# Moving the recurrence's root, scans and operand sums in the mixer stages of a hybrid decoder trunk

## The chip, the core and the metric

The kernel runs on one core of one Trainium2 chip. The time is device time in microseconds from start to end of one execution. In the text PE is the matrix engine, ACT the scalar engine, DVE the vector engine, POOL the general engine (GpSimd) and SP the engine that issues most transfers. PSUM is held in banks of 128 x 512 float32.

## The reference

One layer (DEPTH = 1), 1024 tokens, width 1024, all float32: a norm, two token mixers side by side that are merged by gates, an output projection, then a norm and a squared-ReLU MLP, and a last norm. The change touches the mixers:

```python
h = rms_norm(x, norm_mix)
xa, ga, q, f, v, g, m_a, m_b = split(h @ w_in)
# RG-LRU on blocks of 256 channels
xa = causal_conv4(xa, conv_w, conv_b)
r = sigmoid(xa @ w_r + b_r);  i = sigmoid(xa @ w_i + b_i)
log_a = -8 * r * softplus(-lam);  a = exp(log_a)
u = sqrt(max(-expm1(2 * log_a), 0)) * (i * xa)
h_t = a_t * h_(t-1) + u_t                       # scan over time
y_a = h * gelu(ga)
# HGRN2 on 8 heads of 128, in chunks
q = silu(q);  fg = lb + (1 - lb) * sigmoid(f)
k = (1 - lb) * sigmoid(-f)
o = decayed linear attention(q, k, log fg, v)   # state = decay * state + k v
y_b = rms_norm(o, hg_norm) * silu(g)
y = sigmoid(m_a) * y_a + sigmoid(m_b) * y_b     # then y @ w_out, + x, MLP
```

## The kernel before, in words

Every float32 operand of a product is split into a high part (rounded, by ACT, L87) and a low part (the rest, by DVE, L88), and each product is three matmuls: high by high, low by high and high by low (`mm3`, L130 to L134). A weight tile is loaded by SP (`raw`), split into wH and wL and kept in a ring of six. The splitting of weights is traced with a high priority, so the scheduler of the program places it early on ACT and DVE.

**Stages.** The mixers run in eight stages i = (c, p): two halves of the tokens (c, 512 each) and four pairs of heads (p). `stage(i)` is a generator. Its steps are, in order: the values of the pair before (`v_of(i)`, four blocks tt of 24 matmuls into a bank pv, L350), the projection xa (16 matmul groups in 8 steps), the projection q (8 steps), the first two steps of the projection f, then `rg_lru` (r and i, into banks pr and pi, L430 to L439) and the other six steps of f. A step is six matmuls of 512 columns. `hgrn(i)` holds the attention of stage i and calls `go(n)` between its own blocks on PE, which runs n steps of stage i+1. So the attention of one pair lies between the projections of the next. GO = (24, 5, 1, 1, 2) gives the steps: 24 before the score blocks (own block of 32 matmuls, then after two more steps the blocks of levels 2 and 8, 64 matmuls), 5 before the blocks of 32 and 64, one before the transposes pk of the keys, one before the states pkv (L664), two before the outputs po (L684 to L692). After the last stage `last_stage` has the last values, the projections g and mb, and the transposes of the last output.

**Order.** PE's order in this part is that of the trace (pinned). The order on ACT, DVE and POOL is the scheduler's, fixed when the program is built: each engine runs its own queue strictly in that order.

**Banks.** There are four banks "pj" (all projections, r, i and v), two "sc" and two "hg" (level-8 and 32 scores, pk, pkv, po, the transposes poT of the normalized output and xT_x of the rows of x). A bank is reused when the last reader of its earlier contents is done.

**What the change and the prediction touch.**
- `make_combos` (L303): eight pieces, two in each of stages 4 to 7. POOL forms four sums of the operands (high plus low, L309) and their differences (L313 to L316), ACT copies out the high parts (L322), POOL the low parts (L323), SP stores them. All of it is traced behind `rg_lru`.
- `rg_lru` (L417): sigmoids of r and i on ACT (L424 is the helper that records them, in a fixed order), exp and tanh, then on DVE the product, the root on ACT (L448), two scans on DVE (L456), and one store of 512 KB (L459). The tile xc holds the decay a.
- `q_of` (L461): q times its sigmoid on DVE. `f_of` (L472): the sigmoids f and k (L478, L479); k is scaled by 1 - lb on DVE (L481).
- the end of `hgrn` (L684 to L707): ACT squares each 128 columns of po with a sum (L696) and copies po to `on` (L702); POOL takes the power -0.5 of the mean square (L705, hrs), DVE multiplies `on` by it (L706).
- `on_T` (L369): four transposes of `on` for each head into a bank, scaled by ACT into onT (L376) and stored. It stands at the first v block (tt = 0) two stages later.
- `next_rows` and `transposed` (L296, L158): the four row tiles of the second half of x are loaded, normalized, transposed in stages 1 (after xa), 2, 3 and 4 (third v block), and split into hT10 and hT11 (L87, L88).
- the start of the gates (L1029 to L1044): the first two quads of gate weights are loaded and split, with the loads of the sums t1 and n2 behind the first and T3 and T4 behind the second (`load_combo`); then steps 0 and 3 of both (gX and gZ).

Of the kernel before, what the change touches and what calls it, by code (L numbers as in the profile page):

```python
# [18 lines left out]
P = 128  # L19
# [16 lines left out]
GO = (24, 5, 1, 1, 2)  # L36
# [8 lines left out]
def trunk(ctx: ExitStack, tc: tile.TileContext, x, wts, mlp, pv, gains, mask_f, mask_u, out):  # L45
# [257 lines left out]
    def make_combos(i):  # L303
        k, cut = i // 2, slice(256 * (i % 2), 256 * (i % 2) + 256)
        r = tile_x(f"r{i}").rearrange("p (a b) -> p a b", a=4)
        quarters = ((0, 0), (0, 1), (1, 1), (1, 0))
        for j, (c, h) in enumerate(quarters):
            hi, lo = (hT[c][q][h][:, k, cut].bitcast(F32) for q in range(2))
            ins = G.tensor_tensor(out=r[:, j, :], in0=hi, in1=lo, op=ALU.add)  # L309
            if j == 0:  # L310
                tc.keep_in_program_order(ins)
        b11, b21, b22, b12 = (r[:, j, :] for j in range(4))
        G.tensor_tensor(out=b11, in0=b11, in1=b12, op=ALU.subtract)  # L313
        G.tensor_tensor(out=b12, in0=b22, in1=b12, op=ALU.subtract)
        G.tensor_tensor(out=b22, in0=b11, in1=b22, op=ALU.add)
        G.tensor_tensor(out=b21, in0=b22, in1=b21, op=ALU.subtract)  # L316
        for src, o in ((b11, "t1"), (b22, "n2"), (b12, "T3"), (b21, "T4")):
            if o in ("t1", "T3"):
                st = xt_pool.tile([P, 2, 2, 256], F32, tag="xn", name=f"st{o}{i}", bufs=2)
                at = 0  # L320
            h, lo = (st[:, at, q, :].bitcast(F32R) for q in range(2))
            A.copy(h, src)  # L322
            G.tensor_tensor(out=lo, in0=src, in1=h.bitcast(F32), op=ALU.subtract)  # L323
            nc.sync.dma_start(cd[o][:, :, k, cut], st[:, at])
            at = 1

# [90 lines left out]
    def rg_lru(c, p, xc, xh, xl):  # L417
        wh, wl = next_w()
        nm = f"{c}{p}"
        w, ig, e = (mt(t, f"{t}{nm}", (P, 2, T)) for t in ("rw", "ri", "rr"))  # L420
        last = []
# [25 lines left out]
        V.scalar_tensor_tensor(xc, e, 1.0, w, op0=ALU.add, op1=ALU.mult)  # L447
        on_act(w, w, AF.Sqrt)  # L448
        V.tensor_scalar(xc, xc, -1.0, 1.0, op0=ALU.mult, op1=ALU.add)
        V.scalar_tensor_tensor(w, e, 1.0, w, op0=ALU.add, op1=ALU.mult)  # L450
        V.tensor_tensor(out=ig, in0=ig, in1=w, op=ALU.mult)
        hs = mt("h", f"h{nm}", (P, 2, T))
        for s in range(2):
            u = 2 * p + s
            h = hs[:, s if c == 0 else 1 - s, :]
            V.tensor_tensor_scan(h, xc[:, s, :], ig[:, s, :], hcar[:, u : u + 1], op0=ALU.mult, op1=ALU.add)  # L456
            if c + 1 < NC:
                G.tensor_copy(hcar[:, u : u + 1], h[:, T - 1 : T])
        nc.sync.dma_start(hd[p][:, 2 * c : 2 * c + 2, :], hs)  # L459

    def q_of(c, p, pp):  # L461

        q1 = mt("q1", f"q1{c}{p}", (P, 1536)).rearrange("p (a b) -> p a b", b=3)
        sg = mt("tmp", f"sq{c}{p}", (P, 2, T))
        r2 = lambda a: a.rearrange("p (a b) -> p a b", b=2)
        for s in range(2):
            b = slice(256 * s, 256 * s + 256)
            A.activation(sg[:, s, :], pp[s], AF.Sigmoid)
            V.tensor_tensor(out=q1[:, b, 0:2], in0=r2(sg[:, s, :]), in1=r2(pp[s]), op=ALU.mult)
        return q1  # L470

    def f_of(c, p, pp):  # L472
        ff = mt("f", f"f{c}{p}", (P, 2 * T))
        kk = mt("kk", f"kk{c}{p}", (P, 2 * T))
        for s in range(2):
# [5 lines left out]
            V.tensor_scalar(k, k, omlb[:, u : u + 1], None, op0=ALU.mult)  # L481
# [3 lines left out]
    def hgrn(c, p, got, go):  # L485
        q1, f, kk = got["q1"], got["f"], got["kk"]

        nm = f"{c}{p}"
# [88 lines left out]
        go(GO[0] - 8 * (c + p == 0) - (OWN_BEFORE if c > 0 else 0))  # L577
        pt1 = blocks(kk, lambda k: q1[:, 16 * k : 16 * k + 16, :], "1")
        if c > 0:
            go(OWN_BEFORE)  # L580
# [104 lines left out]
        for s, u in both:  # L685
# [16 lines left out]
            A.copy(on[:, 4 * s : 4 * s + 4, :], po[s].rearrange("p (n d) -> p n d", n=4))  # L702
# [3 lines left out]
        mul(on, on, rs.unsqueeze(2).to_broadcast([P, 8, P]))  # L706
        got["on"] = on  # L707

    gots = [{} for _ in range(NC * NPAIR)]
# [14 lines left out]
    def v_of(i):  # L724
        def between(tt):
            if tt == 0 and i > 1:
                on_T(*where(i - 2), gots[i - 2])
            if tt == 2 and "xn" in gots[i - 1]:
                transposed(gots[i - 1]["xn"], hT[1], i - 1, f"x1{i - 1}")

        yield from v_steps(*where(i - 1), gots[i - 1], between)

    def stage(i):
# [13 lines left out]
        if i == 1:  # L747
            transposed(gots[0]["xn"], hT[1], 0, "x10")
# [8 lines left out]
        for _ in range(2 if i != 1 else 7):  # L757
            next(fs)
            yield
# [4 lines left out]
        yield from rg_lru(c, p, *got["xc"])  # L764
        if i < 4:
            got["xn"] = next_rows(i)
        for k in {4: (0, 1), 5: (2, 3), 6: (4, 5), 7: (6, 7)}.get(i, ()):
            make_combos(k)
# [17 lines left out]
    def last_stage():  # L786
        yield from v_of(NC * NPAIR)
        w = [next_w(), next_w()]
        g2 = []
        for c in range(NC):  # L790
# [3 lines left out]
            for s in range(2):  # L794
                o = g[:, s if c == 0 else 1 - s, :]
                A.activation(o, pp[s], AF.Sigmoid)
                V.tensor_tensor(out=o, in0=o, in1=pp[s], op=ALU.mult)
            yield
# [234 lines left out]
    for q in own[:2]:  # L1033
# [6 lines left out]
        for o in ("t1", "n2") if q == own[0] else ("T3", "T4"):  # L1040
            load_combo(o)
    for step in (0, 3):
        for q in own[:2]:
            gate_step(q, step)  # L1044
    gwork[own[0]]["b"]()
# [376 lines left out]
```

## Time and profile before

| | |
|---|---|
| median of 3 runs | 1621.54 us (1621.21 to 1621.56) |
| the profiled execution | 1626.13 us, its span 1624.3 us |
| PE busy | 1547.5 us, 95% of the span |
| DVE, ACT, POOL busy | 1211.0, 816.2, 148.9 us (75%, 50%, 9%) |
| the mixer stages | 0 to about 611 us of the span |
| DMA | 280.07 MB, mean 172 GB/s |

The profile is of one execution; times inside it are from the start of its span. A row of the timeline gives the start, the length, the engine, the line of the kernel, the operation, out <- in with shapes, and in brackets how long the engine had been idle and what ended that. A row of the waits gives the instruction that waited, what it waited for, and then the sum in us, how often, and the longest. L numbers are lines of the kernel before.

### The profile page before, as it was taken

What the parts mean: (1) busy time and instruction counts of PE and PEld (TensorE: products, weight loads), DVE (VectorE), ACT (ScalarE), POOL (GpSimd) and SP (SyncE); (2) the same over time, 40 slices, a digit from 0 to 9 for tenths busy, and PEclk for the clock granted to TensorE, in tenths of its full rate; (3) what the DMA queues carried; (4) which work ended last, traced back from release to release, by engine and by line L of the source; (5) the groups of instructions that cost most, each with busy time, mean ns of one, the idle gap of its engine ahead of it and who ended that gap; (6) DMA issues with size and microseconds to landing.
All of it is one profiled execution on the core that took longest, in us unless ns stands there. A gap on an engine that the chain in (4) does not pass through costs nothing.

```text
span 1624.3 us, 23115 instructions
## 1 busy us (share of the span) xinstructions
PE 1547.5 (95%) x9072; PEld 1290.7 (79%) x9072; DVE 1211.0 (75%) x1730; ACT 816.2 (50%) x1293; POOL 148.9 (9%) x187
## 2 busy tenths in 40 slices
PE   7999998898988998999999997999999999999998
PEld 6887987787877886888888875788888878888886
DVE  5798676595857744877777379878888898788876
ACT  5655755466564523545444266677766632122113
POOL 1012110516052300000000000000000000000000
PEclk9999999999989899999999999999999999999999
DMA  6323222243332336423236782566666575666652
GB/s 237 104 79 118 84 74 104 70 142 103 112 121 79 130 131 246 156 78 130 78 130 240 266 282 79 218 269 239 246 239 256 231 281 200 260 257 251 260 214 104
DMA packets 71053, 280.07 MB, mean 172 GB/s; under 512 B 7584, under 2 KB 15904, under 8 KB 58016
## 3 DMA queue, kind: packets, MB, share of 16 engines
q1 hardware_dynamic: 67920, 267.58, 44.1%
q10 hardware_dynamic: 3024, 11.01, 1.8%
q8 instruction: 71, 1.16, 0.3%
q14 instruction: 38, 0.31, 0.1%
HBM read 193.63 MB, written 84.93 MB: 171 GB/s over the span
## 4 chain that ended last, share of the span: by engine, by line
PE 76%; DVE 9%; ACT 5%; POOL 4%; issue 3%; DMA 2%; ACTq 0%; POOLq 0%; DVEq 0%; SPq 0%
PE dX L132 4%; PE dX L133 3%; PE dX L134 3%; PE uX L132 3%; PE uX L134 3%; PE uX L133 3%; PE gX L134 3%; PE gX L132 3%; PE gX L133 3%; PE dY L133 2%; PE dY L132 2%; PE dY L134 2%; PE pj_q L132 2%; PE uY L133 2%; PE uY L132 2%
## 5 line engine op out<-in xcount | busy, mean ns | idle before, releaser
L88 DVE TENSOR_TENSOR wL<-raw,wH 128x1024 fp32r<-128x1024 f32 x100 | 123.9, 1239 | 115.4 <-ACT wH L87 113.8
L87 ACT CAST wH<-raw 128x1024 fp32r<-128x1024 f32 x100 | 105.1, 1051 | 89.6 <-PE po L133 37.1
L1331 DVE TENSOR_TENSOR acc<-acc,dX 128x512 f32<-128x512 f32 x128 | 85.0, 683 | 29.5 <-PE dX L134 28.6
L87 ACT CAST wA<-q 128x512 fp32r<-128x512 f32 x46 | 28.5, 621 | 133.7 <-PE dX L134 101.0
L1331 DVE TENSOR_TENSOR acc<-acc,dY 128x512 f32<-128x512 f32 x64 | 43.4, 685 | 15.6 <-PE dY L134 14.5
L134 PE MATMUL po<-wH,y 128*128 128x512 f32 x128 | 50.5, 395 | 0.0
L133 PE MATMUL po<-wL,y 128*128 128x512 f32 x128 | 50.2, 393 | 0.0
L132 PE MATMUL po<-wH,y 128*128 128x512 f32 x128 | 50.1, 392 | 0.0
L1191 ACT ACTIVATE b<-b 128x512 f32<-128x512 f32 x48 | 30.2, 630 | 37.1 <-DVE b L1190 37.1
L155 POOL TENSOR_TENSOR rstd_h<-rstd_h,mhalf 128x1 f32<-128x1 f32 x8 | 5.5, 686 | 396.8 <-DVE rstd_h L154 396.8
L602 POOL TENSOR_SCALAR scT<-dd 32x256 f32<-32x256 f32 x32 | 22.3, 697 | 206.9 <-DVE dd L518 205.4
L88 DVE TENSOR_TENSOR wA<-q,wA 128x512 fp32r<-128x512 f32 x46 | 31.5, 686 | 12.7 <-ACT wA L87 12.5
L402 DVE SCALAR_TENSOR_TENSOR xc<-xp,pvt,xc 128x512 f32<-128x512 f32 x48 | 36.1, 753 | 0.0
L879 DVE TENSOR_TENSOR s<-q,q 128x512 f32<-128x512 f32 x46 | 31.5, 687 | 1.2 <-DMA q<-mlp_in 0.7
L884 DVE TENSOR_TENSOR s<-q 128x512 f32<-128x512 f32 x46 | 31.6, 687 | 0.4
L1192 ACT ACTIVATE b<-b 128x512 f32<-128x512 f32 x48 | 30.0, 630 | 1.1
L132 PE MATMUL pr<-xcH,wH 128*128 128x512 f32 x32 | 14.7, 460 | 16.6 <-ACT rw L424 16.6
L134 PEld LDWEIGHTS po<-wH,y 128*128 128x128 f32 x128 | 24.3, 190 | 5.0
L133 PEld LDWEIGHTS po<-wL,y 128*128 128x128 f32 x128 | 24.2, 189 | 5.1
L132 PEld LDWEIGHTS po<-wH,y 128*128 128x128 f32 x128 | 24.3, 190 | 4.9
L132 PE MATMUL pv<-wH,hT10H 128*128 128x256 f32 x64 | 19.6, 306 | 8.1 <-ACT kk L479 8.1
L134 PE MATMUL uX<-h2B11H,wA 128*128 128x512 f32 x64 | 25.1, 392 | 0.5 <-DVE wA L88 0.5
(2529 smaller groups left out, 5449.1 us busy)
## 6 DMA issues: line engine op xcount, KB each, us to landing
raw<-wts_in SPq DMA_DIRECT2D x96, 512.0 KB, 3.4
q<-mlp_in SPq DMA_DIRECT2D x92, 512.0 KB, 3.5
y<-yd SPq DMA_DIRECT2D x7, 1024.0 KB, 8.3
x<-x_in SPq DMA_DIRECT2D x8, 512.0 KB, 6.0
hd<-h SPq DMA_DIRECT2D x8, 512.0 KB, 2.8
od<-onT ACTq DMA_DIRECT2D x8, 512.0 KB, 2.6
cdT<-stT SPq DMA_DIRECT2D x16, 256.0 KB, 2.7
o<-od SPq DMA_DIRECT2D x4, 1024.0 KB, 6.3
```

Of the source, the lines that this page charges most:

```text
L87: keep(A.copy(h, src))
L88: keep(V.tensor_tensor(out=lo, in0=src, in1=h.bitcast(F32), op=ALU.subtract))
L132: pin(PE.matmul(o, ah, bh, start=first, stop=False, **how))
L133: pin(PE.matmul(o, ah, bl, start=False, stop=False, **how))
L134: pin(PE.matmul(o, al, bh, start=False, stop=last, **how))
L402: V.scalar_tensor_tensor(xc[:, s, :], xp[:, j : j + T], pvt[:, PV_CW + 8 * j + u : PV_CW + 8 * j + u + 1], xc[:, s, :], op0=ALU.mult, op1= ...
L602: G.tensor_scalar(scT[32 * b : 32 * b + 32, :, 32 * b : 32 * b + 32], dd[32 * b : 32 * b + 32, :, :], 1.0, 0.0, op0=ALU.mult, op1=ALU.add,)
L879: V.tensor_tensor(out=sa[:, 0, :], in0=a21, in1=a22, op=ALU.add)
L884: V.tensor_tensor(out=sb[:, 0, :], in0=a21, in1=a11, op=ALU.add)
L1191: A.activation(b[:, at, :], b[:, at, :], AF.Relu, scale=-1.0 if at == 2 else 1.0)
L1192: A.activation(b[:, at, :], b[:, at, :], AF.Square)
L1331: V.tensor_tensor(out=dst, in0=dst, in1=banks[bk, pr], op=op)
```

## The change

- `rg_lru` writes the decay into a tile of its own (a) and leaves the root, the product with it, the scans (now in place) and the stores (two of 256 KB) to a function `tail`. It is called in the next stage: behind the first v block, or in stage 1 behind xa.
- `make_combos` becomes a generator of two parts, sums and copies; the parts are called after xa and after `rg_lru` in stages 4 to 7, and in the last stage.
- GO starts with 26 in place of 24, and in every stage but the first the own block is alone, two steps ahead of the other two.
- f runs four steps ahead of `rg_lru` in place of two.
- q is scaled by 1 - lb, in the instruction that multiplies it by its sigmoid; the scaling of k is gone.
- ACT writes `on` from po, scaled by the power, in eight instructions (Identity, 128 columns each); the copy of po and DVE's product are gone.
- `on_T` stands at the second v block (tt = 1); the row tiles 1, 2 and 3 are transposed in stage 2 (third v block) and stage 3 (first and third).
- The sums t1, n2, T3 and T4 are loaded behind both first quads, and the first gate steps are pinned.

```diff
@@ -33,7 +33,7 @@
 OUT_TILES = 8
 QUADS = 16
 LEVELS = (2, 8)
-GO = (24, 5, 1, 1, 2)
+GO = (26, 5, 1, 1, 2)
 OWN_BEFORE = 2
 
 
@@ -314,15 +314,26 @@
         G.tensor_tensor(out=b12, in0=b22, in1=b12, op=ALU.subtract)
         G.tensor_tensor(out=b22, in0=b11, in1=b22, op=ALU.add)
         G.tensor_tensor(out=b21, in0=b22, in1=b21, op=ALU.subtract)
+        yield
         for src, o in ((b11, "t1"), (b22, "n2"), (b12, "T3"), (b21, "T4")):
             if o in ("t1", "T3"):
                 st = xt_pool.tile([P, 2, 2, 256], F32, tag="xn", name=f"st{o}{i}", bufs=2)
                 at = 0
             h, lo = (st[:, at, q, :].bitcast(F32R) for q in range(2))
-            A.copy(h, src)
+            ins = A.copy(h, src)
+            if o == "t1":
+                tc.keep_in_program_order(ins)
             G.tensor_tensor(out=lo, in0=src, in1=h.bitcast(F32), op=ALU.subtract)
             nc.sync.dma_start(cd[o][:, :, k, cut], st[:, at])
             at = 1
+        yield
+
+    pieces = [make_combos(i) for i in range(8)]
+    piece_parts = [pieces[n // 2] for n in range(16)]
+
+    def combos_on(n):
+        for _ in range(n):
+            next(piece_parts.pop(0))
 
     def project_steps(c, name):
 
@@ -414,10 +425,11 @@
         split(xc, xh, xl)
         return xc, xh, xl
 
-    def rg_lru(c, p, xc, xh, xl):
+    def rg_lru(c, p, got, xc, xh, xl):
         wh, wl = next_w()
         nm = f"{c}{p}"
         w, ig, e = (mt(t, f"{t}{nm}", (P, 2, T)) for t in ("rw", "ri", "rr"))
+        a = mt("h", f"a{nm}", (P, 2, T))
         last = []
 
         def on_act(*a, **k):
@@ -444,19 +456,21 @@
             on_act(w[:, s, :], w[:, s, :], AF.Tanh, scale=sp4[:, u : u + 1])
         V.tensor_tensor(out=ig, in0=ig, in1=xc, op=ALU.mult)
         V.tensor_scalar(w, w, 0.0, None, op0=ALU.max)
-        V.scalar_tensor_tensor(xc, e, 1.0, w, op0=ALU.add, op1=ALU.mult)
-        on_act(w, w, AF.Sqrt)
-        V.tensor_scalar(xc, xc, -1.0, 1.0, op0=ALU.mult, op1=ALU.add)
-        V.scalar_tensor_tensor(w, e, 1.0, w, op0=ALU.add, op1=ALU.mult)
-        V.tensor_tensor(out=ig, in0=ig, in1=w, op=ALU.mult)
-        hs = mt("h", f"h{nm}", (P, 2, T))
-        for s in range(2):
-            u = 2 * p + s
-            h = hs[:, s if c == 0 else 1 - s, :]
-            V.tensor_tensor_scan(h, xc[:, s, :], ig[:, s, :], hcar[:, u : u + 1], op0=ALU.mult, op1=ALU.add)
-            if c + 1 < NC:
-                G.tensor_copy(hcar[:, u : u + 1], h[:, T - 1 : T])
-        nc.sync.dma_start(hd[p][:, 2 * c : 2 * c + 2, :], hs)
+        V.scalar_tensor_tensor(a, e, 1.0, w, op0=ALU.add, op1=ALU.mult)
+        V.tensor_scalar(a, a, -1.0, 1.0, op0=ALU.mult, op1=ALU.add)
+
+        def tail():
+            A.activation(w, w, AF.Sqrt)
+            V.scalar_tensor_tensor(w, e, 1.0, w, op0=ALU.add, op1=ALU.mult)
+            V.tensor_tensor(out=ig, in0=ig, in1=w, op=ALU.mult)
+            for s, u in us:
+                h = ig[:, s, :]
+                V.tensor_tensor_scan(h, a[:, s, :], h, hcar[:, u : u + 1], op0=ALU.mult, op1=ALU.add)
+                if c + 1 < NC:
+                    G.tensor_copy(hcar[:, u : u + 1], h[:, T - 1 : T])
+                nc.sync.dma_start(hd[p][:, (s, 3 - s)[c], :], h)
+
+        got["tail"] = tail
 
     def q_of(c, p, pp):
 
@@ -466,7 +480,10 @@
         for s in range(2):
             b = slice(256 * s, 256 * s + 256)
             A.activation(sg[:, s, :], pp[s], AF.Sigmoid)
-            V.tensor_tensor(out=q1[:, b, 0:2], in0=r2(sg[:, s, :]), in1=r2(pp[s]), op=ALU.mult)
+            u = 2 * p + s
+            V.scalar_tensor_tensor(
+                q1[:, b, 0:2], r2(sg[:, s, :]), omlb[:, u : u + 1], r2(pp[s]), op0=ALU.mult, op1=ALU.mult
+            )
         return q1
 
     def f_of(c, p, pp):
@@ -478,14 +495,13 @@
             A.activation(f, pp[s], AF.Sigmoid)
             A.activation(k, pp[s], AF.Sigmoid, scale=-1.0)
             V.tensor_scalar(f, f, omlb[:, u : u + 1], lb[:, u : u + 1], op0=ALU.mult, op1=ALU.add)
-            V.tensor_scalar(k, k, omlb[:, u : u + 1], None, op0=ALU.mult)
         V.tensor_scalar(ff, ff, F_MIN, 1.0, op0=ALU.max, op1=ALU.min)
         return ff, kk
 
     def hgrn(c, p, got, go):
         q1, f, kk = got["q1"], got["f"], got["kk"]
 
-        nm = f"{c}{p}"
+        nm, first = f"{c}{p}", c + p == 0
         mul = lambda o, a, b: V.tensor_tensor(out=o, in0=a, in1=b, op=ALU.mult)
         dd = mt("dd", f"dd{nm}", (P, 8, 32))
 
@@ -574,9 +590,9 @@
         t4 = nxt.rearrange("p (a b) -> p a b", b=4)
         q4 = qb.rearrange("p a (b c) -> p a b c", c=c1)
         level_q(q4, t4, g1, c1)
-        go(GO[0] - 8 * (c + p == 0) - (OWN_BEFORE if c > 0 else 0))
+        go(GO[0] - (10 if first else OWN_BEFORE))
         pt1 = blocks(kk, lambda k: q1[:, 16 * k : 16 * k + 16, :], "1")
-        if c > 0:
+        if not first:
             go(OWN_BEFORE)
         pt2 = blocks(kb, lambda k: qa[:, k * g0 // 32 : (k + 1) * g0 // 32, 1:7, :], str(c0))
         pt8 = blocks(kc, lambda k: q4[:, k * g1 // 32 : (k + 1) * g1 // 32, 1:7, :], str(c1), "hg")
@@ -699,13 +715,16 @@
                     AF.Square,
                     accum_out=ssq[:, 4 * s + n : 4 * s + n + 1],
                 )
-            A.copy(on[:, 4 * s : 4 * s + 4, :], po[s].rearrange("p (n d) -> p n d", n=4))
         V.tensor_scalar(ssq, ssq, 1.0 / P, EPS, op0=ALU.mult, op1=ALU.add)
         rs = mt("hrs", f"hrs{nm}", (P, 8), bufs=2)
         G.tensor_tensor(out=rs, in0=ssq, in1=mhalf, op=ALU.pow)
-        mul(on, on, rs.unsqueeze(2).to_broadcast([P, 8, P]))
+        for s, _ in both:
+            for n in range(4):
+                j = 4 * s + n
+                A.activation(on[:, j, :], po[s][:, n * P : (n + 1) * P], AF.Identity, scale=rs[:, j : j + 1])
         got["on"] = on
 
+    xn1 = {}
     gots = [{} for _ in range(NC * NPAIR)]
     where = lambda i: divmod(i, NPAIR)
 
@@ -723,10 +742,12 @@
 
     def v_of(i):
         def between(tt):
-            if tt == 0 and i > 1:
+            if tt == 0:
+                gots[i - 1]["tail"]()
+            if tt == 1:
                 on_T(*where(i - 2), gots[i - 2])
-            if tt == 2 and "xn" in gots[i - 1]:
-                transposed(gots[i - 1]["xn"], hT[1], i - 1, f"x1{i - 1}")
+            for n in {(2, 2): (1,), (3, 0): (2,), (3, 2): (3,)}.get((i, tt), ()):
+                transposed(xn1[n], hT[1], n, f"x1{n}")
 
         yield from v_steps(*where(i - 1), gots[i - 1], between)
 
@@ -745,7 +766,10 @@
             pinned[0] = True
         yield
         if i == 1:
-            transposed(gots[0]["xn"], hT[1], 0, "x10")
+            gots[0]["tail"]()
+            transposed(xn1[0], hT[1], 0, "x10")
+        if i > 4:
+            combos_on(2)
 
         def convolve():
             got["xc"] = conv(c, p, xc, xps)
@@ -754,18 +778,18 @@
         got["q1"] = q_of(c, p, pq)
         yield
         fs = hooked(project_steps(c, f"f{c}{p}"), {6: convolve} if i == 1 else {})
-        for _ in range(2 if i != 1 else 7):
+        for _ in range(4 if i != 1 else 7):
             next(fs)
             yield
         if i == 1:
             pf = yield from fs
             got["f"], got["kk"] = f_of(c, p, pf)
             yield
-        yield from rg_lru(c, p, *got["xc"])
-        if i < 4:
-            got["xn"] = next_rows(i)
-        for k in {4: (0, 1), 5: (2, 3), 6: (4, 5), 7: (6, 7)}.get(i, ()):
-            make_combos(k)
+        yield from rg_lru(c, p, got, *got["xc"])
+        for n in ((0,), (1,), (2, 3))[i] if i < 3 else ():
+            xn1[n] = next_rows(n)
+        if i > 3:
+            combos_on(1 if i == 4 else 2)
         if i != 1:
             pf = yield from fs
             got["f"], got["kk"] = f_of(c, p, pf)
@@ -785,6 +809,7 @@
 
     def last_stage():
         yield from v_of(NC * NPAIR)
+        combos_on(2)
         w = [next_w(), next_w()]
         g2 = []
         for c in range(NC):
@@ -795,6 +820,8 @@
                 o = g[:, s if c == 0 else 1 - s, :]
                 A.activation(o, pp[s], AF.Sigmoid)
                 V.tensor_tensor(out=o, in0=o, in1=pp[s], op=ALU.mult)
+            if c == 0:
+                combos_on(1)
             yield
         w = [next_w(), next_w()]
         for c in range(NC):
@@ -1037,11 +1064,13 @@
         if q == own[0]:
             gwork[q]["sums"]()
         gwork[q]["d"]()
-        for o in ("t1", "n2") if q == own[0] else ("T3", "T4"):
-            load_combo(o)
+    for o in ("t1", "n2", "T3", "T4"):
+        load_combo(o)
+    pinned[0] = True
     for step in (0, 3):
         for q in own[:2]:
             gate_step(q, step)
+    pinned[0] = False
     gwork[own[0]]["b"]()
     live["g2"] = gp_tile("b", "g2_0")
     nc.sync.dma_start(live["g2"], g2d)
```

## The prediction

> **What bounds the kernel now.** I read the busy shares first, then the waits of PE, then the granted clock around the longest waits, then the engine each wait names.
>
> ```profile
> PE 1547.5 (95%) x9072; PEld 1290.7 (79%) x9072; DVE 1211.0 (75%) x1730; ACT 816.2 (50%) x1293; POOL 148.9 (9%) x187
> ```
> ```profile
> PE pr L132 <- ACT rw L424: 16.6, 4, 4.2
> ...
> PE pv L132 <- ACT kk L479: 8.1, 4, 2.8
> PE pj_xa L133 <- DVE hT10L L88: 7.0, 1, 7.0
> ...
> PE pj_q L132 <- issue: 4.4, 2, 3.8
> ...
> PE gZ L132 <- ACT onT L376: 2.2, 1, 2.2
> ```
>
> PE is the bound: 95% busy, so a change pays only by what it takes out of PE's idle time or puts in. The waits (total us, times, longest) that lie in the mixers are 16.6 + 8.1 + 7.0 + 3.8 = 35.5 us. Each also costs something after it ends:
>
> ```profile
> 149.00:155.00 6.00, 6.00 (x16) 4.72 (x17) 4.69 (x11) 0.94 (x2) 0.00 (x0) 0.56 0.03 13
> 269.30:274.00 4.70, 4.70 (x12) 3.68 (x13) 2.36 (x10) 0.00 (x0) 0.00 (x0) 0.52 0.00 0
> 314.00:318.50 4.50, 4.50 (x13) 3.56 (x14) 0.00 (x0) 1.68 (x3) 4.42 (x8) 0.62 0.57 200
> 336.20:340.30 4.10, 4.08 (x34) 4.08 (x35) 4.07 (x6) 2.64 (x6) 0.00 (x0) 1.00 0.45 181
> ...
> 455.60:461.50 5.90, 5.90 (x14) 4.64 (x15) 0.00 (x0) 1.68 (x3) 5.74 (x9) 0.50 0.50 178
> 477.90:482.00 4.10, 4.10 (x22) 4.10 (x23) 4.10 (x5) 2.59 (x6) 0.00 (x0) 0.58 0.43 174
> ...
> 549.50:553.60 4.10, 4.10 (x22) 4.10 (x23) 4.10 (x7) 2.61 (x6) 0.00 (x0) 0.59 0.23 90
> ```
>
> These are the stretches behind the gaps (window and its length, busy times of PE, its weight load, DVE, ACT, POOL; the column ahead of the last two is the granted clock). Behind the 3.8 us issue gap PE loses 6.00 × 0.44 = 2.6 us, behind the 7.0 us gap 4.70 × 0.48 = 2.3. Behind a pr gap it loses 5.90 × 0.50 = 2.95 (455.60), behind the first of them 4.50 × 0.38 = 1.7 (314.00). Of the four pv gaps one cost no clock (336.20), two cost 4.10 × 0.42 = 1.7 each, and the one left is taken like them.
>
> Why the four pr gaps: ACT runs its queue in order. One of them, as PE has it and then as ACT and POOL have it:
>
> ```profile
> 455.59 0.79 PE L132 MATMUL pr<-xcH,wH 128*128 128x512 f32 x1 [4.13 <-ACT rw L424]
> ```
> ```profile
> 447.40 0.28 ACT L696 ACTIVATE on<-po 128x128 f32<-128x128 f32 x1
> ...
> 448.32 0.22 ACT L696 ACTIVATION_READ_ACCUMULATOR on<-po 128x1 f32 x1
> 448.57 0.59 ACT L702 COPY on<-po 128x512 f32<-128x512 f32 x1
> 452.95 0.40 ACT L322 CAST stt<-r 128x256 fp32r<-128x256 f32 x1 [3.79 <-POOL r L313]
> ...
> 454.86 0.68 ACT L424 ACTIVATE rw<-pr,pvt 128x512 f32<-128x512 f32 x1
> ```
> ```profile
> 448.89 1.65 POOL L705 TENSOR_TENSOR hrs<-hssq,mhalf 128x8 f32<-128x8 f32 x1 [9.15 <-DVE hssq L703]
> ```
>
> The copies of the operand sums (L322) wait for POOL, and the sigmoid that frees the pr bank (L424) stands behind them until 454.86. The pv gaps have the root ahead of what frees the f bank:
>
> ```profile
> 545.18 1.28 ACT L424 ACT_TABLE_LOAD   x1
> 546.48 1.06 ACT L424 ACTIVATE rw<-rw 128x1024 f32<-128x1024 f32 x1
> 547.55 1.28 ACT L479 ACT_TABLE_LOAD   x1
> 548.85 0.60 ACT L479 ACTIVATE kk<-pj_f 128x512 f32<-128x512 f32 x1
> ```
>
> **What goes.** The sums' copies are traced behind the sigmoids, so the pr waits go: 16.6 us, and the clock after them, 1.7 for the first and 2.95 taken for the other three, 10.5: 27.1 us. The root follows the next chain: 8.1, and three times 1.7: 13.2. The transposes of row tile 3 go one stage earlier, so the 7.0 us wait at stage 4's xa goes with its 2.3: 9.3. The 3.8 us "issue" wait names no releaser and comes after a long run of score blocks; that run is now cut by two steps, and I take it as gone, with its 2.6: 6.4 (none to all; the trace cannot say more). Together **56.0 us**.
>
> **What comes.** (a) Normalization moves from two ACT copies and a DVE product to eight ACT scalings that read PSUM and wait for POOL's power. Let E be when the second po bank is done, 447.35 above (447.40 is the first square on it). The squares end 1.2 later, the power at 450.54, 3.2 after E. ACT then has, ahead of the pr sigmoid, eight scalings of 128x128. No row has that form: a quarter of the 512-wide copy is 0.15, a square and its READ add up to 0.50 (0.28 + 0.22), and four such pairs, overlapped, took 447.40 to 448.54, 0.28 each. I take 0.2 to 0.28, nearest to the pairs: 1.6 to 2.25 us. With the sigmoid's 0.68 the bank is free at E + 5.5 to 6.1. PE wanted it at 451.46 (455.59 less 4.13), E + 4.1. So six stages (2 to 7) stall 1.5 to 2.1 us with the 0.05 from sigmoid to PE; 1.9 taken. The clock loss of 1.7 behind such a gap is taken half the time, 0.85 each. 6 × (1.9 + 0.85) = 16.5 us (6 × 1.5 = 9 to 6 × 3.9 = 23.4).
>
> By the Trainium skill, TensorE: Matmul & The Clock Gate, Part 1, the clock falls only after an idle window of some 3.4 us. By that, (a) would be 5.1 us less and the time about 1601; the row at 477.90 disagrees, 0.58 behind a gap that was at most 2.8, and decides; this gets no chance of its own.
>
> (b) Scores now come two steps of 1.4 us later (GO 26 for 24), so pk follows the end of q's projection, and the copies kT stand behind q's sigmoids.
>
> ```profile
> 507.59 0.58 ACT L634 COPY scT<-sc 64x512 f32<-64x512 f32 x1 [0.33 <-PE sc L628]
> 509.51 0.48 ACT L659 COPY kT<-pk 128x384 f32<-128x384 f32 x1 [1.34 <-PE pk L654]
> ...
> 513.85 1.05 ACT L87 CAST wH<-raw 128x1024 fp32r<-128x1024 f32 x1
> ```
> ```profile
> L664 PE MATMUL pkv<-v,kT x12: 270/275/356, 511.0 to 512.3; 128*128 128x128 f32 x12
> ```
>
> After the scT copy (508.1) ACT now has a table load 1.28, a sigmoid (0.60 long as at 548.85, 0.5 to the next start), a wH cast 0.95, a sigmoid 0.5, then kT 0.48: 511.8, where PE wanted pkv at 511.0. That is 0.8 in hgrn 1 to 3; in 4 to 6 ACT also waits in that stretch for a POOL sum, 1.45; 0.5 in hgrn 7: 2.4 + 4.4 + 0.5 = 7.3 us (0 to 12, with the clock). By the Trainium skill, ScalarE: Activation LUTs, What ACT_TABLE_LOAD costs, a switch is 2.66 us with its drain; by that, (b) would be 7 × 1.38 = 9.7 more and the time about 1615. The rows 545.18 to 546.48 show 1.30 to the next operation and decide; this too gets no chance of its own.
>
> (c) Row tile 2 is now transposed in stage 3 between the first and second v blocks, into both hg banks; poT follows one v block later and needs such a bank. It is free when DVE has written the low parts, which stand in DVE's order behind the whole f chain and now also behind the second half of the recurrence.
>
> ```profile
> 254.92 2.46 DVE L456 TENSOR_TENSOR_SCAN h<-xc,hcar,ri 128x512 f32<-128x512 f32 x2
> 257.29 0.53 DVE L480 TENSOR_SCALAR f<-f,par 128x512 f32<-128x512 f32 x1
> ...
> 263.44 1.23 DVE L88 TENSOR_TENSOR wL<-raw,wH 128x1024 fp32r<-128x1024 f32 x1
> ...
> 268.46 0.70 DVE L88 TENSOR_TENSOR hT10L<-xT_x,hT10H 128x512 fp32r<-128x512 f32 x1
> ...
> 269.39 0.70 DVE L88 TENSOR_TENSOR hT11L<-xT_x,hT11H 128x512 fp32r<-128x512 f32 x1
> ```
> ```profile
> 258.08 1.03 PE L162 MATMUL xT_x<-ident,xn 128*128 128x128 f32 x8
> ```
>
> In before the low parts of tile 3, in the same place a stage later, ended 12.0 us after their transpose (258.08 to 270.1) and 12.8 after the last f operation (257.29). Now two wL (2.5) leave that stretch, and a product, another and the two scans (1.2 + 1.2 + 2.46) enter it: 15.2. The step of PE's time is this:
>
> ```profile
> 608.06 0.39 PE L132 MATMUL mb<-hT11H,wH 128*128 128x512 f32 x1
> 608.29 0.39 PE L133 MATMUL mb<-hT11L,wH 128*128 128x512 f32 x1
> ```
>
> 0.23 a matmul. After E come the second bank's po matmuls and one f step (1.8 to r), 24 matmuls of r and i (5.5), four f steps of six (5.5), two v blocks of 24 half-width matmuls (2.8 each), a transpose (0.9, half of it beside them) and the stall of (a): PE wants poT at about E + 20.5. ACT ends r and i's last sigmoid near E + 9.5, then a table load 1.28, four sweeps of 0.63, a load 1.28, f, k, f with a wH: f at E + 17, so DVE is done at E + 32.5. **12 us** and 2.5 of clock: 14.5 (0, if DVE gets there early, to 16).
>
> (d) The gates. In before t1 and n2 (4 MB) came in while the last projections ran; now all 8 MB of sums follow, on SP's queue, the second quad's load, which waits for a tile that DVE frees.
>
> ```profile
> DMA  0000000899999992000027699999999991019500
> GB/s 0 0 0 0 0 0 10 207 378 408 439 413 418 418 416 96 28 5 0 0 111 290 252 315 423 403 429 424 418 434 418 424 429 71 10 43 373 229 0 0
> ```
> ```profile
> 614.04 0.50 PE L132 MATMUL gZ<-hT01H,wA1234H 128*128 128x512 f32 x1 [2.22 <-ACT onT L376]
> ```
> ```profile
> 615.68 0.69 DVE L88 TENSOR_TENSOR wA<-q,wA 128x512 fp32r<-128x512 f32 x1 [2.83 <-ACT wA L87]
> ```
>
> (40 slices of 580 to 645.) The first step is pinned on wA, ready at 616.4, where before gZ could start at 614.0: 2.4 later. 8.5 MB from 616.4 at about 0.42 MB/us is done by 637 to 639; four pinned steps of 2.7 us hold PE until 627, and the other steps want each operand at about the time it lands. I take +2 us (−1.5 to 6).
>
> **At nothing:** the scaled q (0.05 longer) for the k product gone (2 × 0.48) and the normalizing product gone: about 2 us a stage off DVE, which is 75% busy and off PE's path but in (c); the scan in place and two stores of 256 KB for one of 512, and three row loads of 512 KB a stage earlier on SP, in stretches like 455 to 482 above where DMA is at 0.50 or under; the power's place on POOL, 9% busy. Were DVE's cover gone it would cost those 2 us a stage back. f's two further steps before r stand against two fewer after it, no sum.
>
> Sum of what comes: 16.5 + 7.3 + 14.5 + 2 = **40.3**. Net −15.7 on the profiled execution, 1626.1 to 1610.4. That execution lies 4.6 above the median of the runs, 1621.5, so **1606 us**, −1.0%.
>
> **Rivals.**
> - *The scalings hold the pr banks as long as the sums did* (slower). ACT is in order; if each scaling costs 0.4 to 0.45 rather than 0.2 to 0.28 (the pair of a square and its READ adds up to 0.50), or a wH cast of 1.05 falls between them, the sigmoid ends at E + 7.5 or later. The stall is then 3.6 and the clock loss 2.95 in six stages: 39.3 for 16.5, +22.8: 1629. It decides against the change from 15.7 / 6 = 2.6 us a stage, clock included, over what (a) has. For it: the clock rows; against: 0.28 for such a pair, start to start.
> - *The gates wait for DMA.* If the sums come one after another behind the quad, T3 and T4 would be 5 us late each, with a clock loss: +10, 1616. For it: 0.42 MB/us is the top of the GB/s row. Against: the pinned steps give 10.8 us of cover.
> - *(c) is cheap.* If the f chain runs early, since two wL and 1 us of k products are gone, the wait falls under 2 us: 1593. Against: the 7.0 row is the same wait with less ahead of it.
> - *The gaps stay.* The change does not do what it says if the "issue" wait remains (6.4), (b) drops the clock each time (5) and the pv banks still come late (5): +16, 1622, no change.
>
> **How the numbers follow.** Chances: forecast 0.48 (its own range 1598 to 1613), scalings slow 0.19, gates 0.12, (c) cheap 0.11, gaps stay 0.10. To leave no more than 2 in 10 out, the range goes from 1593 to 1627. A measurement of this kernel can tell about 0.2%, 3.2 us, from no change: faster takes the forecast, the gates, cheap (c), 0.71; same most of the last, 0.08; slower the scalings and the rest, 0.21.
>
> **What would show it.** PE's waits should have no pr wait on L322's place of over 3 us, no pv wait on kk, none at pj_xa; instead pr waits of 1.6 to 2.2 six times, pkv on kT 0.5 to 1.5 seven times, one poT wait of about 12 on hT10L or hT11L, and the gates' first wait near 4.5. It is wrong if the pr waits reach 3.6, if poT does not wait, or if gY or gX wait for transfers.

## The result and the profile after

The changed kernel takes 1645.57 us (median of 4 runs, 1641.66 to 1647.95) against 1621.55 for the kernel before beside it: a ratio of 1.0146 (95% interval 1.0126 to 1.0166), 24 us slower. 1606 was forecast. The profiled execution took 1646.05 us, its span is 1644.3. PE is busy 1549.7 us of it (1547.5 before), so 18 of the 20 us by which the span grew are idle time of PE; the mean granted clock is 0.979 in both profiles.

PE's waits in the changed kernel (what waited, for what: us in total, times, longest):

```profile
PE poT L386 <- DVE hT10L L88: 12.4, 1, 12.4
PE pr L132 <- ACT rw L436: 11.3, 6, 1.9
...
PE sc L644 <- ACT qf L612: 7.5, 3, 2.7
...
PE sc L633 <- DVE qb L505: 5.1, 3, 3.9
...
PE gX L132 <- ACT wA L87: 3.8, 1, 3.8
PE pj_xa L134 <- DVE wL L88: 3.5, 2, 1.8
PE xT_x L162 <- ACT onT L387: 3.4, 1, 3.4
PE pk L670 <- DVE dd L534: 2.6, 1, 2.6
PE pk L670 <- DVE kk L505: 2.3, 2, 1.9
...
PE pkv L680 <- ACT kT L675: 1.9, 3, 0.7
PE g L134 <- DVE wL L88: 1.8, 1, 1.8
```

What the change was to remove is gone: no pr wait of 4 us, no pv wait on kk, none of xa on hT10L, and the issue wait is at most 1.0. What was forecast to come is there as well: pr six times 1.9, poT 12.4, the gates 3.8. But four kinds of waits stand here that the forecast did not have: the scores of 32 and 64 (sc) on qb and qf, the keys' transposes on kk, the next projection on wL, together 7.5 + 5.1 + 2.3 + 3.5 + 1.8 = 20.2 us, and xT_x on onT, 3.4. The one wait of the keys' transposes on dd also grew, from 1.0 to 2.6. Windows behind three of the waits (the granted clock is ahead of the last two columns):

```profile
183.60:188.00 4.40, 4.40 (x12) 3.49 (x13) 0.00 (x0) 1.20 (x2) 0.00 (x0) 0.61 0.04 14
...
212.70:219.00 6.30, 6.30 (x34) 6.30 (x35) 1.46 (x8) 1.37 (x2) 0.00 (x0) 0.59 0.31 125
400.40:404.00 3.60, 3.60 (x16) 2.98 (x17) 0.00 (x0) 1.98 (x3) 0.00 (x0) 1.00 0.04 14
449.00:457.00 8.00, 6.00 (x29) 4.93 (x30) 7.23 (x12) 7.43 (x12) 4.36 (x6) 0.57 0.32 100
```

Behind one pr wait of 1.9 us the clock was low (183.60, 4.40 × 0.39 = 1.7 us lost), behind another it was not (400.40); of the six it was low behind three. The poT wait cost 6.30 × 0.41 = 2.6 behind it; the last window, with a sc wait of 2.4 us in it, has a clock of 0.57.

The new waits begin in DVE. This is its timeline in stage 5, then POOL's and ACT's (start, length):

```profile
439.90 3.28 DVE L413 SCALAR_TENSOR_TENSOR xc<-xp,pvt,xc 128x512 f32<-128x512 f32 x3
...
445.67 2.09 DVE L505 TENSOR_TENSOR qb<-qb,seg 128x256 f32<-128x256 f32 x2
447.68 1.21 DVE L505 TENSOR_TENSOR kk<-kc,seg 128x512 f32<-128x512 f32 x1
448.82 1.20 DVE L505 TENSOR_TENSOR qf<-qb,seg 128x512 f32<-128x512 f32 x1
```
```profile
444.89 1.46 POOL L309 TENSOR_TENSOR r<-hT10H,hT10L 128x256 f32<-128x256 f32 x1
...
448.42 1.05 POOL L315 TENSOR_TENSOR r<-r 128x256 f32<-128x256 f32 x1
```
```profile
449.51 0.40 ACT L323 CAST stt<-r 128x256 fp32r<-128x256 f32 x1 [11.54 <-POOL r L315]
...
450.34 0.61 ACT L612 COPY qf<-qb 128x512 f32<-128x512 f32 x1
```

The sums on POOL now run beside the score chain on DVE, and both are slow. The same two instructions of the score chain and the conv, in stages 4 to 7 (count: shortest/median/longest in ns, first and last start), before and after:

```profile
L489 DVE TENSOR_TENSOR qf<-qb,seg x4: 675/683/690, 359.6 to 573.6; 128x512 f32<-128x512 f32 x4
...
L402 DVE SCALAR_TENSOR_TENSOR xc<-xp,pvt,xc x18: 727/742/884, 356.6 to 509.3; 128x512 f32<-128x512 f32 x18
...
L315 POOL TENSOR_TENSOR r<-r x7: 723/734/738, 320.9 to 534.2; 128x256 f32<-128x256 f32 x7
```
```profile
L505 DVE TENSOR_TENSOR qf<-qb,seg x4: 678/1204/1215, 375.8 to 597.1; 128x512 f32<-128x512 f32 x4
...
L413 DVE SCALAR_TENSOR_TENSOR xc<-xp,pvt,xc x18: 743/1079/1229, 365.9 to 521.9; 128x512 f32<-128x512 f32 x18
...
L315 POOL TENSOR_TENSOR r<-r x8: 730/1052/1610, 330.0 to 588.8; 128x256 f32<-128x256 f32 x8
```

683 ns became 1204, 742 became 1079, POOL's 734 became 1052. All of DVE is busy 1218.3 us, against 1211.0 before, although the change takes 24 instructions off it. In before most of the sums ran right behind the outputs po, in a stretch where DVE had next to nothing to do (0.93 us busy of 4.2 in the pr gap at 451).

### The profile page after: what moved, and what is told of

It is laid out like the page before. It is cut to its first block, busy times and chain, and to the rows that moved or that the text cites. A ratio compares the mean times of both kernels' runs of the same rounds, so it can differ in the third digit from the quotient of the medians.

```text
span 1644.3 us, 23134 instructions
## 1 busy us (share of the span) xinstructions
PE 1549.7 (94%) x9072; PEld 1287.7 (78%) x9072; DVE 1218.3 (74%) x1706; ACT 819.9 (50%) x1341; POOL 190.6 (12%) x187
## 4 chain that ended last, share of the span: by engine, by line
PE 70%; DVE 13%; ACT 6%; POOL 5%; issue 4%; DMA 2%; ACTq 0%; DVEq 0%; POOLq 0%; SPq 0%
PE dX L132 3%; PE dX L133 3%; PE dX L134 3%; PE uX L132 3%; PE uX L134 3%; PE uX L133 3%; PE gX L133 3%; PE gX L132 3%; PE gX L134 3%; PE dY L134 2%; PE dY L133 2%; PE dY L132 2%; PE uY L134 2%; PE uY L132 2%; PE uY L133 2%
## 5 line engine op out<-in xcount | busy, mean ns | idle before, releaser
L1360 DVE TENSOR_TENSOR acc<-acc,dY 128x512 f32<-128x512 f32 x64 | 43.3, 685 | 15.6 <-PE dY L134 14.5
L326 POOL TENSOR_TENSOR stt<-r,stt 128x256 fp32r<-128x256 f32 x16 | 35.3, 2211 | 90.6 <-ACT stt L323 90.6
L712 ACT ACTIVATE on<-po 128x128 f32<-128x128 f32 x64 | 16.8, 276 | 48.4 <-PE po L708 48.4
L413 DVE SCALAR_TENSOR_TENSOR xc<-xp,pvt,xc 128x512 f32<-128x512 f32 x48 | 40.4, 862 | 0.0
L323 ACT CAST stt<-r 128x256 fp32r<-128x256 f32 x16 | 6.4, 403 | 47.6 <-POOL r L315 47.5
L134 PEld LDWEIGHTS po<-wH,y 128*128 128x128 f32 x128 | 24.0, 188 | 4.9
```

The source lines that it names most:

```text
L134: pin(PE.matmul(o, al, bh, start=False, stop=last, **how))
L413: V.scalar_tensor_tensor(xc[:, s, :], xp[:, j : j + T], pvt[:, PV_CW + 8 * j + u : PV_CW + 8 * j + u + 1], xc[:, s, :], op0=ALU.mult, op1= ...
L1360: V.tensor_tensor(out=dst, in0=dst, in1=banks[bk, pr], op=op)
```

## The experiments

Theory: the sums beside the score chain are the main loss, and the poT wait the second. Rivals: the recurrence's tail lengthens the chain; the order on ACT (a sum's copy that waits for POOL ahead of qf); the two steps of GO. Times are medians; since the runs of before beside the experiments differ (medians 1622.6 to 1624.7), ratios to those beside each are given, and a difference of 0.0100 is 16.2 us.

### The transposes put back in order

```diff
-            if tt == 1:
+            if tt == 0 and i > 1:
                 on_T(*where(i - 2), gots[i - 2])
-            for n in {(2, 2): (1,), (3, 0): (2,), (3, 2): (3,)}.get((i, tt), ()):
+            for n in {(2, 2): (1,), (3, 2): (2,)}.get((i, tt), ()):
...
+        if i == 3:
+            transposed(xn1[3], hT[1], 3, "x13")   # behind xa
```

> The changed kernel with the transposes put back in order: poT at the first v block again, row tile 2 at the third v block of stage 3, row tile 3 behind the xa of stage 3. Theory (the hg banks wait for DVE's low parts): the 12.4 us poT wait and its 13.65 us at half clock (6.8 lost) go, and the 3.4 us wait of xT_x on onT in stage 2 with 1.7 of clock: 1646 falls to about 1622. Rival (the low parts are late wherever they stand): the wait moves to the score block that takes the next hg bank, and only 5 to 10 us are won, 1636 to 1641.

1627.06 us, ratio 1.0013 (1.0002 to 1.0024): 21.6 us less than the changed kernel, of the 24 expected. Its waits have no poT on hT10L; part came back in the scores, whose waits on qb and qf add up to 15.6 us for 12.8:

```profile
PE sc L633 <- DVE qb L505: 9.1, 3, 4.0
...
PE poT L386 <- ACT on L724: 2.7, 2, 1.4
...
PE xT_x L162 <- ACT onT L387: 0.5, 1, 0.5
```

So the order of the transposes is worth about 21 us, and the low parts need not be late wherever they stand. (The 6.8 us of clock in the expectation counts all 13.65 us of low clock, in most of which PE was idle; what PE lost behind the wait is the 2.6 worked out above.)

### POOL's sums left out

The four sums, the four differences and the four low parts of each piece are left out; a DMA fills the tile that the copies read, and both halves stored are the high part.

```diff
-            ins = G.tensor_tensor(out=r[:, j, :], in0=hi, in1=lo, op=ALU.add)
+            nc.sync.dma_start(r[:, j, :], hi)
...
-        G.tensor_tensor(out=b11, in0=b11, in1=b12, op=ALU.subtract)   # and three more
...
-            G.tensor_tensor(out=lo, in0=src, in1=h.bitcast(F32), op=ALU.subtract)
```

> The changed kernel without POOL's work for the operand sums: the tile that the copies read is filled by DMA with one high part, the low parts are not made, and both stored halves are the high part (that part of the computation is left out). Theory (in stages 4 to 7 the sums now run beside the score chain, and POOL and DVE slow each other): DVE's 128x512 products, 1.2 us in that stretch, fall to 0.7, the waits sc on qb 5.1 and qf 7.5, pk on kk 2.3, pj_xa and g on wL 5.3 go with some 10 us of clock: about 1616 to 1620. Rival (the recurrence's tail in the score chain is what makes it late): the waits on qb and wL stay, at most 8 us are won, 1638.

1618.30 us, ratio 0.9963 (0.9950 to 0.9976): 29.7 us less. DVE's instructions stand in the same order as in the changed kernel, and last as they did before:

```profile
L499 DVE TENSOR_TENSOR qf<-qb,seg x4: 684/687/690, 372.2 to 565.7; 128x512 f32<-128x512 f32 x4
...
L407 DVE SCALAR_TENSOR_TENSOR xc<-xp,pvt,xc x18: 729/741/749, 365.8 to 502.8; 128x512 f32<-128x512 f32 x18
```

All waits of sc, wL and kk are gone from the list but 0.3 us on qf; poT 12.4 and pr 11.3 stand as in the changed kernel. DVE's 1706 instructions are busy 1185.6 us in all, where the changed kernel's 1706 are busy 1218.3: POOL's part lengthened them by 33 us. The tail, the two steps and the new place of the own block are all in this kernel, so without POOL's part they do not make the scores late, alone or together.

### Each POOL operation a copy of one operand

Same places, same order on every engine, but each sum, difference and low part is a copy, so that part of the computation is left out.

```diff
-            ins = G.tensor_tensor(out=r[:, j, :], in0=hi, in1=lo, op=ALU.add)
+            ins = G.tensor_copy(r[:, j, :], hi)
```

> The changed kernel with each of POOL's sums, differences and low parts made a copy of one operand, in the same places and order (that part of the computation is left out). If any POOL work beside DVE slows DVE as the sums do: the conv instructions stay near 1.05 us and the products qf near 1.08, 1638 to 1646. If it is POOL's reading of two operands, or its length, that does it (theory): conv falls towards 0.76, qf towards 0.7, the sc and wL waits shrink by half or more, 1620 to 1632.

1620.04 us, ratio 0.9973 (0.9961 to 0.9984): 28 less, nearly as if POOL did nothing.

```profile
L505 DVE TENSOR_TENSOR qf<-qb,seg x4: 686/878/879, 373.6 to 570.7; 128x512 f32<-128x512 f32 x4
...
L413 DVE SCALAR_TENSOR_TENSOR xc<-xp,pvt,xc x18: 727/812/927, 366.1 to 504.3; 128x512 f32<-128x512 f32 x18
...
L309 POOL COPY r<-hT01H x7: 394/397/591, 369.6 to 560.4; 128x256 f32<-128x256 f32 x7
```

A copy is 0.40 us long when undisturbed, the sum 0.73. DVE's products are still 0.2 us longer than 0.68, but no score waits more than 0.3 us for them. So POOL work beside DVE is not harmful as such. Whether what harms is that the sums are longer, or that they read two operands, this run does not tell.

### The order on ACT alone

Each copy of a sum is placed on ACT behind the exp and tanh sweeps of the last recurrence traced, so none of that recurrence's stage stands ahead of the copy of qf.

```diff
             ins = A.copy(h, src)
-            if o == "t1":
-                tc.keep_in_program_order(ins)
+            if rg_done:
+                how = mybir.DependencyInfo(mybir.DependencyClass.NoSync, mybir.DependencyReason.DATA)
+                tc.add_manual_dep(ins.ins, rg_done[-1].ins.name, how, reason="rg_done")
...
+        rg_done.append(last[-1])   # rg_lru, behind the sweeps
```

> The changed kernel with the sums where they are on POOL, but their copies held on ACT behind the recurrence's sweeps of their own stage, so that none stands ahead of the copy of qf. If the order on ACT is the loss: the qf waits of 7.5 us go with half of the clock and the rest with them, 1622 to 1628. If POOL beside DVE is the larger part (theory): qb, wL and kk waits stay, qf waits on DVE instead by about 1 each: 1632 to 1640.

1645.11 us, ratio 1.0140 (1.0123 to 1.0157): nothing won. The scores' waits on qf and qb are gone but 0.6 us, and the loss is at the next place where DVE's work is wanted:

```profile
PE pj_xa L134 <- DVE wL L88: 9.5, 2, 5.0
...
PE g L134 <- DVE wL L88: 4.9, 1, 4.9
PE pk L674 <- DVE kk L509: 4.8, 4, 1.6
```

The qf products are at 0.68 us again, but the sums lengthen others: DVE is busy 1227.3 us in all. The same splitting of a weight, here and then without POOL's part:

```profile
427.76 1.74 DVE L88 TENSOR_TENSOR wL<-raw,wH 128x1024 fp32r<-128x1024 f32 x1
```
```profile
418.43 1.25 DVE L88 TENSOR_TENSOR wL<-raw,wH 128x1024 fp32r<-128x1024 f32 x1
```

Neither range was met, the order's least of all: in the changed kernel it decides where the loss shows, not how large it is.

### The tail put back, and GO at 24

```diff
-        got["tail"] = tail
+        tail()
```

> The changed kernel with the root and the scans traced inside the recurrence again, all else as changed. Rival (the tail in the score chain makes sc late): the sc waits of 12.6 us and their clock, some 22 in all, go, pv on kk comes back with 13, and the poT wait shrinks by 5 to 8: about 1629. Theory (POOL beside DVE makes sc late): the sc waits stay within 4 us, pv on kk comes back: 1646 to 1653.

1638.72, ratio 1.0092 (1.0077 to 1.0107), between the two: 8.8 less.

```profile
PE sc L644 <- ACT qf L612: 7.5, 3, 2.7
...
PE poT L386 <- DVE hT10L L88: 5.1, 1, 5.1
PE pv L132 <- ACT kk L496: 4.9, 5, 1.3
```

The qf waits stay to the tenth, and those on qb add up to 5.4 for 5.1, so the tail does not make them; what it costs is poT, 12.4 against 5.1, and the wait on dd (2.6), which is not in this list.

```diff
-GO = (26, 5, 1, 1, 2)
+GO = (24, 5, 1, 1, 2)
```

> The changed kernel with GO back at 24, the joined score block two steps earlier, all else as changed. The conv of the next stage (six DVE instructions) is traced at step 6 of q: with 26 it comes ahead of the block of 32, with 24 behind it. Theory (POOL beside DVE): the sc waits fall by a third to a half, since less of DVE's work lies ahead, but stay: 1636 to 1642. Rival (the two steps are the cause): they vanish with their clock, 1620 to 1626.

1637.96, ratio 1.0084 (1.0069 to 1.0099). The time fits the theory, and the scores' waits fall by half (6.3 on qb, none on qf). But the theory did not have what else came: the pr waits fall from 11.3 to 3.3, and the keys' transposes wait on ACT, whose copy of scT (from 440.07) stands behind the copy of a sum that waits for POOL:

```profile
PE pk L670 <- ACT scT L649: 22.8, 3, 8.2
```
```profile
439.76 0.41 ACT L323 CAST stt<-r 128x256 fp32r<-128x256 f32 x1 [9.70 <-POOL r L315]
```

PE idles about as long as in the changed kernel (93.4 us of the span for 94.6); the 9072 matmuls are busy 7 us less.

### One part alone in the kernel before

The sums in their new places, nothing else (the copy of t1 kept in the order of the trace, as in the changed kernel):

```diff
-        for k in {4: (0, 1), 5: (2, 3), 6: (4, 5), 7: (6, 7)}.get(i, ()):
-            make_combos(k)
+        if i > 3:
+            combos_on(1 if i == 4 else 2)   # and behind xa, and in the last stage
```

> The kernel before with one part of the change alone: the operand sums in two parts in their new places. If the sums' place brings what it takes away (theory): the pr waits of 16.6 us and their clock of 10.5 go, and waits of scores and of the keys' transposes on DVE's chain and on the copies of scT come in, in stages 5 to 8, of about the same size: 1616 to 1628. If POOL beside DVE costs nothing here (rival): 1621 less 27, some 1595 to 1600.

1635.11 us, ratio 1.0068 (1.0051 to 1.0084): 11 us slower than before and worse than expected. The pr wait is left once (4.2) of four times, and

```profile
PE pk L665 <- ACT scT L644: 21.9, 3, 7.7
...
PE sc L510 <- DVE qb L500: 8.3, 1, 8.3
```

came in, the first again behind the copy of a sum that waited 9.69 us for POOL: the sums' place alone loses more than it wins. The root, scans and stores behind the next chain, nothing else:

```diff
-        on_act(w, w, AF.Sqrt)
...
+        got["tail"] = tail
...
+            if tt == 0:
+                gots[i - 1]["tail"]()
```

> The kernel before with the root, the scans and their stores alone moved behind the next score chain's start. Theory (the f chain of DVE is what the first score blocks and the low parts wait for once 5 us more stand in it): pv waits of 8.1 us go with 5.1 of clock, the wait at xa of stage 4 grows by 4 to 6, and the block of level 8 waits 1 to 3 us a stage: 1618 to 1634. Rival (DVE has room, 75% busy): only the gain is left, 1608.

1617.82 us, ratio 0.9972 (0.9959 to 0.9985): 4.5 us won, neither the rival's 13 nor a loss. The pv waits are gone; xa's wait, which was to grow by 4 to 6, stays 7.0, and others come in (beside the one shown, 2.6 on v and 2.3 on dd):

```profile
PE pk L657 <- DVE kk L492: 4.4, 4, 1.4
```

### Mending

Normalization as before (two ACT copies and DVE's product), the rest as changed:

```diff
+            A.copy(on[:, 4 * s : 4 * s + 4, :], po[s].rearrange("p (n d) -> p n d", n=4))
...
-                A.activation(on[:, j, :], po[s][:, n * P : (n + 1) * P], AF.Identity, scale=rs[:, j : j + 1])
+        mul(on, on, rs.unsqueeze(2).to_broadcast([P, 8, P]))
```

> The changed kernel with the normalization alone as before. Theory: the six pr waits of 11.3 us in all go, with 5 of clock; DVE's product of 1.2 us a stage costs nothing or up to 1 where DVE's chain is late: 1629 to 1634. Rival (the next thing on ACT is as late, as the 1.17 us that ACT idles behind the first two sigmoids is all there is): under 5 won, 1641 and more.

1629.70, ratio 1.0034 (1.0020 to 1.0047): 18 less, in the range expected. The six pr waits are gone, one longer came in, and the 3.4 us wait of xT_x on onT is gone as well:

```profile
PE pr L132 <- ACT rw L436: 5.0, 1, 5.0
```

Transposes in order and the sums ahead of the score chain:

```diff
-        if i > 4: combos_on(2)          # behind xa
+        if i > 4: combos_on(1)
...
-            combos_on(1 if i == 4 else 2)   # behind the recurrence
+            combos_on(3)
```

> The changed kernel with the transposes in order (as in the run of the transposes) and the sums ahead of the score chain: three of four parts behind the recurrence, the last copies behind the next xa. Theory (the sums beside the block of 32 and its DVE chain are the loss): the sc, wL and kk waits go, 1627 less 22 to 28: 1599 to 1606. Rival (POOL beside DVE costs the same wherever it stands): the waits move to the f chain and to the first score blocks, 1620 to 1628.

1617.57, ratio 0.9960 (0.9945 to 0.9975): 8.6 us less than with the transposes alone, a third of the 22 to 28 expected. The scores' waits on qb and qf are down from 15.6 to 2.7 us, but the sums now stand beside the f chain, DVE is busy 1217.1 us, and other waits stand (2.4 on kk and 3.1 on v with the transposes alone; g on the same copy 1.6 in both):

```profile
PE pk L670 <- DVE kk L505: 4.6, 3, 1.6
PE pj_xa L132 <- ACT v L375: 4.4, 3, 1.6
```
All of it, with normalization (the edit above) and gates as before:

```diff
-    for o in ("t1", "n2", "T3", "T4"):
-        load_combo(o)
-    pinned[0] = True
...
+        for o in ("t1", "n2") if q == own[0] else ("T3", "T4"):
+            load_combo(o)
```

> As the run with the sums ahead, and also the normalization as before (two ACT copies and a DVE product) and the start of the gates as before. Theory (the scalings hold the pr banks 1.9 us six times, with 1.7 of clock in three; the gates' order costs 2): 14 to 18 less than the run with the sums ahead, 1582 to 1590. Rival (the sigmoid would be as late behind the wH cast and the copies): within 5 of that run.

1621.71, ratio 0.9982 (0.9973 to 0.9992): a clear miss. Without the scalings the copy of a sum stands ahead of the pr sigmoid again, as in the kernel before:

```profile
PE pr L132 <- ACT rw L436: 20.0, 4, 5.0
```
```profile
454.29 0.41 ACT L323 CAST stt<-r 128x256 fp32r<-128x256 f32 x1 [5.30 <-POOL r L315]
454.61 0.68 ACT L436 ACTIVATE rw<-pr,pvt 128x512 f32<-128x512 f32 x1
```

The scalings, it seems, had held the sums' copies back. With the copies held behind the sweeps by the explicit order shown above:

> As the run with everything mended (transposes in order, sums ahead, normalization and gates as before), and the sums' copies held behind the recurrence's sweeps on ACT, so that none stands ahead of the pr sigmoid. Theory: the four pr waits of 20.0 us and the clock behind them (6.83 at half three times and 3.41 once, 12 lost) go: 1588 to 1594, faster than before by 2%. Rival (the sums' work makes another wait as long, the f bank or the values): 1605 to 1615.

1596.83 us, ratio 0.9848 (0.9833 to 0.9862): 25 us faster than the kernel before and 48 faster than the changed one, 3 us above the range expected. But for 10.2 us at the very start, as before, only small waits are left in the mixers:

```profile
PE sc L637 <- DVE qb L509: 5.3, 3, 1.8
PE pj_xa L132 <- ACT v L378: 4.7, 3, 1.6
...
PE pk L674 <- DVE dd L538: 2.6, 1, 2.6
PE pkv L684 <- ACT kT L679: 2.5, 6, 0.7
```

## Why the prediction was wrong

- **What goes**, 56.0 us: the waits in it (35.5 us) went; only 1.0 us of issue is left. Right. The rest, 20.5 us of clock, cannot be told from the clock behind the waits that came: the mean is 0.979 in both profiles.
- **(a) the scalings**: six waits of 1.9, 11.3 in all, as worked out; the clock was low behind three of the six, which is the half that was taken. Right. That taking the scalings out won 18, near the 16.5 put down, is in part luck: a pr wait of 5.0 came in there, and the 3.4 of xT_x went.
- **(b) kT**: 1.9 for 7.3, and without POOL's sums 3.9, six times 0.7 at most: the further wait of 0.6 that I put down for stages 4 to 6 is not there. Too large.
- **(c) poT**: 12.4 and 2.6 of clock for 12 and 2.5. Right in place and size. What was not in it: xT_x waits for onT in stage 2 (3.4), which falls to 0.5 with the transposes in order and goes with the normalization as before. In all the order of the transposes cost 21.6 for 14.5.
- **(d) the gates**: first wait 3.8 for 4.5, and none that names a transfer. Right as far as the waits tell; no run has the gates alone.
- **"At nothing"** is the step that failed. It held DVE, 75% busy, to be off PE's path, and never asked what the sums' new place does: the step was looked at on ACT's queue only (the copies behind the sigmoids), not on POOL's, where twelve instructions a piece were moved, most of them from a stretch in which DVE rests into the one in which it makes the scores. So the forecast had no term for it. The runs show one: POOL and DVE lengthen each other by 1.4 to 1.8 times, the chain comes late, and sc, wL and kk wait, 20.2 us and their clock. Leaving POOL's part out won 29.7.

Of the rivals, the slower one (each scaling 0.4 us and more) was not it: the pr waits stayed at 1.9. None named POOL beside DVE. Nor did the three signs of being wrong come true (pr waits of 3.6, poT not waiting, gates waiting for transfers): they tested the terms that the sum had, not the one that it lacked.

The Trainium skill states the rule that was needed, SBUF — State Buffer, under SBUF: two separate sides: DVE with two operands in SBUF and a POOL operation that reads SBUF share one pair of ports, and whichever comes second is shut out for the whole instruction. The rows agree that the two hold each other up: 683 ns to 1204 beside sums that are 734 long alone, and 878 beside copies of 394. At 425.89 one of POOL's low parts took 7.09 us while DVE's instructions kept their usual times (the splitting of a weight 1.22); where both lengthen, 1204 is less than 683 + 734, so those rows do not show that one waits out the whole of the other.

What stays open: the two runs (29.7 and 21.6 less, each alone) add up to 27.6 below before, where the forecast without (c) stood at 30; that they add was not run. How much of the clock's loss belongs to which wait was not taken apart either. Whether two operands or the mere length on POOL harms was not told apart.

## What to carry to other kernels

A step that is moved must be looked at on every engine that it issues to, and against what the others do in its new place: an idle engine is not free to use when its instructions lengthen those of the engine beside it. A wait that goes from an in-order queue shows where the next late thing stands; here an explicit order for the sums' copies won 22 us once the other causes were mended, and nothing before that.

## What was not expected of the hardware

POOL's 128x256 sum is 0.73 us alone and 1.05 beside DVE, and a low part of the same size took 7.09 us (at 425.89) and 7.10 (at 497.69) while DVE ran without a break; DVE's 128x512 product with two operands is 0.68 alone and 1.20 beside sums, 0.88 beside copies of 0.40. DVE's instructions of one operand lengthen too: the 128x1024 step that turns a into 1 - a in place is 0.69 us in stages 4 to 7 without POOL's part and 1.23 in the changed kernel (medians of four). Behind a PE gap of 1.9 us the granted clock was low in three stages (0.61 over 4.40 us at 183.60) and full in the three others, so half the price, as it was put down, is an average and not a rule.
